# Fetching a norm weight's row on ScalarE's queue, with a buffer of ones for the first filling products

## The chip, the cores and the metric

The kernel runs on one core of a Trainium2 chip. The metric is the device time in microseconds of one execution, the median of several runs. A profile of one execution gives the times of single instructions, in microseconds from the start of its span.

## The reference

One step of a streaming encoder layer for 2048 new frames and 64 frames of a running stream, each of 1024 features. What matters here is its beginning, a norm and one wide projection:

```python
def rms_norm(x, g):
    xf = x.astype(jnp.float32)
    y = xf * lax.rsqrt(jnp.mean(xf * xf, axis=-1, keepdims=True) + EPS)
    return (y * g.astype(jnp.float32)).astype(x.dtype)
...
    aq, ak, av, ag, hq, hf, hi, hg = jnp.split(rms_norm(x, ln_g) @ w_in, SPLITS, axis=-1)
...
    o_a = attn_fn(heads(aq), k, v).reshape(B, T, W_A) * jax.nn.silu(ag)
    o_b, S = hgrn2_branch(hq, hf, hi, hg, lb, norm_g, s0)
    y = x + jnp.concatenate([o_a, o_b], axis=-1) @ w_out
```

Half of the projected features go through chunked attention, half through a gated linear recurrence. A second projection adds to the input, and a last norm follows. All data is 32 bits wide.

## The kernel before, in words

The frames are worked on in four blocks of 512 (the second carries the 64 frames of the running stream as well). For each block, the normed input is transposed into features by frames, split into a high part `xh` and a rest `xl`, and multiplied with 32 column groups of the input weights, each split likewise. The attention and the recurrence of a block run between its projections; the output projection follows at the end.

The order of every engine is written out by a planner in the kernel (`Plan`): a main program for TensorE yields after each product or two, and threads (loads, norms, splits, attention) go on when the planner's own clock `C.now` has reached the time that they wait for. The planner's clock only decides the order in which instructions are written; it isn't a time on the chip. Each engine executes its own list in order and waits on semaphores. Most instructions are recorded by one helper at line 266, so the profile is read by tiles.

The change lies in `program()`, in the first dozen microseconds:

- VectorE clears `g_in` (128 partitions by 1024), then SyncE fetches the input norm's weights, one row of 4 KB, into its first partition. The list of first loads stands in lines 2064 to 2074: two tiles of frames `xn` (128 by 1024, 512 KB each), the row, the first weights `wraw`, a third tile, the second weights, the fourth tile (in the room `kd`), the 4 KB of bounds `lbg`, and the third and fourth weights (in `kd` and `v`).
- Two products with a matrix of ones (lines 2112 to 2114) spread the row over all 128 partitions, one half into the bank `s` and one into the bank `pv`: the other partitions of `g_in` hold zeros, so the sum over partitions is the row.
- `x_tile` (line 542) takes the squares of a tile on ScalarE, makes the scale `rstd` of each frame there, scales the tile on VectorE by it and by the spread row (one half with `s`, one with `pv`), transposes its eight pieces on TensorE with the identity `ident`, four to a bank (`acc`, `tr`, `g`); `x_split` casts them into `xh` on ScalarE and puts the rest into `xl` on VectorE.
- GpSimd casts the first weights and takes their rests (`w<-wraw`), two column blocks at a time.
- `project` (line 732) multiplies: eight products of `xh` with the weights, eight of `xl` with them, eight of `xh` with the weights' rest.
- Until the row and the first tiles are there, TensorE is given filling products into the bank `g`, whose values are never read: `spinning()` (line 2101), seven ahead of the row and one wherever the planner finds nothing else (lines 2108 to 2118).

`C.breath` is a 128 by 128 buffer that GpSimd clears between long rows of its work, as a pause.

Of the kernel before, what the change touches and what calls it, by code (L numbers as in the profile page):

```python
# [8 lines left out]
F32 = mybir.dt.float32  # L9
# [8 lines left out]
P = 128  # L18
# [354 lines left out]
def hymba_step(  # L373
# [23 lines left out]
    nc = tc.nc  # L397
    C = Plan()
    act, dve, pool, pe, sp = (Queue(C, e, x) for e, x in (("A", nc.scalar), ("D", nc.vector), ("P", nc.gpsimd),
                                                          ("T", nc.tensor), ("S", nc.sync)))  # L400
# [4 lines left out]
    cst = ctx.enter_context(tc.tile_pool(name="cst", bufs=1))  # L405
# [7 lines left out]
    def T(pool_, shape, dt, tag, **kw):  # L413
        uid[0] += 1
        C.name(homes.get(id(pool_), ""), tag, kw.get("bufs") or 1, f"{tag}_{uid[0]}")
        return pool_.tile(list(shape), dt, tag=tag, name=f"{tag}_{uid[0]}", **kw)

    def psum(tag, shape=(P, 512), bufs=1):
        return T(ps, shape, F32, tag, bufs=bufs)
# [27 lines left out]
                                     ck=1, slot=4, x4=0, x5=0, rec=1).items()}  # L447


    ident = T(cst, [P, P], F32, "ident")  # L450
    make_identity(nc, ident)
    ones = T(cst, [P, P], F32R, "ones")
    mask = T(cst, [P, P], U32, "mask")
    eps_t = T(cst, [P, 1], F32, "eps")
    one_t = T(cst, [P, 1], F32, "one")
    C.breath = T(cst, [P, P], F32, "breath")
    reset = T(cst, [P, 512], F32, "reset")
    asb = [T(cst, [P, 4, P], F32, f"asb{i}") for i in range(2)]
    g_norm = T(cst, [P, NHB], F32, "gnorm")
# [54 lines left out]
    g_in = T(px, [P, D], F32, "gin")  # L514
# [16 lines left out]
    def x_rows(sb, c, rows):  # L531
        if c < WIN:
            tok = SUPER[sb][0] + c
            return x_prompt[tok : tok + rows, :]
        return x_sample[:rows, :]
# [1514 lines left out]
    def program():  # L2050
# [13 lines left out]
        for what, i in (("x", 0), ("x", 1), ("g", 0), ("w", 0), ("x", 2), ("w", 1), ("x", 3), ("b", 0), ("w", 2),  # L2064
                        ("w", 3)):
            if what == "g":
                sp.dma_start(g_in[0:1], ln_in_g.rearrange("(o d) -> o d", o=1))
            elif what == "b":
                sp.dma_start(lbg, lb_gamma)
            elif what == "x":  # L2070
                sp.dma_start(xr0[i], x_rows(0, i * P, P))
            else:
                sp.dma_start(wr0[i], w_in[order[i][1]].rearrange("p (k n) -> p k n", k=KT))
            landed[what, i] = C.dma()
        for i in range(4):
            raws[i] = (wr0[i], landed["w", i], "raw" if i < 2 else None)
        spin = psum("g")
# [1 line left out]
        tk["g"].take()  # L2079
        tk["s_ps"].take()  # L2080
        tk["pv"].take()
        C.now = 600.0
        C.free["P"] = 4000.0

        def first_x():
# [12 lines left out]
            yield lambda: 3 in w_at  # L2098
            tk["kv"].put()

        def spinning():
            pe.matmul(spin[:, :P], ident, ident, start=True, stop=True)
            C.now += 200.0

        C.spawn(first_x(), 0)
        C.spawn(forget_bounds(), 1)
        C.spawn(weights(), 2)
        for _ in range(7):
            spinning()
            yield None  # L2110

        for a in range(2):
# [1 line left out]
            yield None  # L2114
        have.add("gain")
        while "rows" not in have:
            spinning()
            yield None
        tk["g"].put()

# [1 line left out]
        for sb in range(nsb):  # L2122
# [6 lines left out]
            for u, (kind, g) in enumerate(JOBS[sb]):  # L2129
# [11 lines left out]
                if (kind[0], g) not in made:  # L2141
                    d, evs = made[kind[0], g] = (head_jobs if kind[0] == "h" else pair_jobs)(sb, g)
# [98 lines left out]
    def out_rows_a():  # L2241
# [12 lines left out]
        wo_load(6, halves_of(hi, lo))  # L2254

    C.main(program())
    C.drain()

# [57 lines left out]
```

## Time and profile before

| | |
|---|---|
| median of 3 runs | 1248.94 us (1248.63 to 1250.27) |
| the profiled execution | 1248.92 us |
| its span (first to last instruction) | 1247.2 us |
| TensorE busy | 1231.4 us, 99% of the span |
| VectorE, ScalarE, GpSimd busy | 887.9, 701.3, 371.6 us |
| first product of the projection | 12.39 us from the span's start |

In the profile PE is TensorE and PEld its weight loads, DVE is VectorE, ACT is ScalarE, POOL is GpSimd and SP is SyncE; SPq and ACTq are DMA issues of these two. A filling or a transposing product of 32-bit data is one `pe` call. In the profile a filling product and each half of the spreading show as two instructions (the seven calls are 14).

### The profile page before, as it was taken

Reading aid. Unit: us, or ns where it says so; the run is one execution under the profiler, and the core shown is the slowest. Engines: PE = TensorE matmul, PEld = TensorE weight load, DVE = VectorE, ACT = ScalarE, POOL = GpSimd, SP = SyncE. Lnnn points to the kernel's source line nnn. Section 1 sums busy time; section 2 is a strip of 40 time slices with the busy share of each in tenths; the row PEclk is TensorE's granted clock in tenths of the full one; section 3 lists DMA queues with packets and bytes.
Section 4 is the critical chain, followed back from the end, with each engine's and each line's share of the span. In section 5 each row is a group of like instructions: output and inputs, shape, how many; then the busy total and the mean of one; then the engine's idle time right before and its main releaser. Section 6 shows DMA issues by size and latency. Waiting matters only on the chain.

```text
span 1247.2 us, 22061 instructions
## 1 busy us (share of the span) xinstructions
PE 1231.4 (99%) x8060; PEld 1078.6 (86%) x8060; DVE 887.9 (71%) x1862; ACT 701.3 (56%) x1535; POOL 371.6 (30%) x698
## 2 busy tenths in 40 slices
PE   8999999999999999999999999999999999999997
PEld 7788887999999999998888888898888888888786
DVE  6678778776857678687584748683848574787886
ACT  6354546666656557575565657763636455643443
POOL 6757565111120210202533535100101204441110
PEclk9999999999999999999999999999999999999999
DMA  7788688635454554636859596846363656897331
GB/s 266 265 309 287 226 328 330 242 131 211 141 187 143 181 203 143 219 126 228 282 205 344 201 359 226 276 163 213 127 234 115 216 209 263 311 318 202 127 136 68
DMA packets 95406, 273.29 MB, mean 219 GB/s; under 512 B 10369, under 2 KB 43137, under 8 KB 77634
## 3 DMA queue, kind: packets, MB, share of 16 engines
q1 hardware_dynamic: 95154, 271.62, 61.9%
q8 instruction: 64, 1.05, 0.3%
q14 instruction: 44, 0.36, 0.1%
q10 hardware_dynamic: 144, 0.26, 0.1%
HBM read 188.23 MB, written 85.19 MB: 219 GB/s over the span
## 4 chain that ended last, share of the span: by engine, by line
PE 77%; DVE 5%; issue 2%; ACT 2%; DMA 1%; POOL 1%; SPq 0%; DVEq 0%; ACTq 0%; POOLq 0%
PE acc L266 55%; PE g L266 7%; PE tr L266 5%; PE pv L266 5%; PE s L266 5%; DVE xn L266 1%; DVE pr L266 1%; DMA xn<-in_x_prompt_dram 1%; DMA wraw<-in_w_in_dram 0%; POOL w L266 0%; ACT ck L266 0%; DVE q L266 0%; DVE mixa L266 0%; DVE k L266 0%; ACT sig L266 0%
## 5 line engine op out<-in xcount | busy, mean ns | idle before, releaser
L266 PE MATMUL acc<-xh,w 128*128 128x512 f32 (+2 forms) x2688 | 567.1, 349 | 1.7 <-ACT sig L266 0.8
L266 PEld LDWEIGHTS acc<-xh,w 128*128 128x128 f32 x2688 | 434.3, 189 | 52.7 <-DVE gq L266 1.1
L266 PE MATMUL acc<-xl,w 128*128 128x512 f32 (+2 forms) x1344 | 296.1, 350 | 0.0
L266 PEld LDWEIGHTS acc<-xl,w 128*128 128x128 f32 x1344 | 217.2, 189 | 24.7
L266 DVE CUSTOM_DVE_ANT_0 pr<-s,bias 128x640 f32<-128x640 f32 (+5 forms) x144 | 100.8, 704 | 34.2 <-PE s L266 33.7
L266 ACT ACTIVATE pr<-pr,nm 128x640 f32<-128x640 f32 (+4 forms) x132 | 100.7, 763 | 41.3 <-DVE nm L266 40.4
L266 ACT CAST ph<-tr 128x512 fp32r<-128x512 f32 (+3 forms) x176 | 88.3, 508 | 62.8 <-PE tr L266 33.7
L266 POOL TENSOR_TENSOR w<-wraw,w 128x256 fp32r<-128x256 f32 x120 | 105.2, 906 | 57.3 <-issue 22.4
L266 POOL TENSOR_TENSOR mixa<-mixa,sga 128x256 f32<-128x256 f32 (+1 forms) x36 | 28.2, 784 | 308.1 <-DVE mixa L266 266.9
L266 DVE TENSOR_TENSOR ph<-tr,ph 128x512 fp32r<-128x512 f32 (+3 forms) x176 | 100.6, 590 | 8.8 <-ACT ph L266 7.6
L266 PE MATMUL pv<-ph,v 128*128 128x256 f32 (+2 forms) x344 | 95.7, 370 | 0.5 <-DVE ph L266 0.5
L266 PE MATMUL tr<-ident,pr 128*128 128x128 f32 x580 | 90.6, 273 | 0.4 <-DVE sig L266 0.2
L266 PEld LDWEIGHTS tr<-ident,pr 128*128 128x128 f32 x580 | 71.0, 140 | 13.6 <-issue 2.2
L266 ACT ACTIVATE sig<-acc 128x256 f32<-128x256 f32 (+2 forms) x86 | 42.7, 497 | 61.8 <-PE acc L266 61.6
L266 DVE TENSOR_SCALAR pr<-pr,sm 128x640 f32<-128x640 f32 (+4 forms) x132 | 72.2, 547 | 4.7
L266 ACT COPY vT<-acc 128x512 f32<-128x512 f32 (+2 forms) x62 | 31.0, 500 | 75.6 <-PE acc L266 75.4
L266 DVE TENSOR_TENSOR mixa<-mixa,pv 64x256 f32<-64x256 f32 (+1 forms) x144 | 56.9, 395 | 21.0 <-ACT mixa L266 16.7
L266 PEld LDWEIGHTS pv<-ph,v 128*128 128x128 f32 x344 | 58.3, 189 | 7.2 <-DVE ph L266 0.9
L266 ACT ACTIVATE sig<-sig 128x512 f32<-128x512 f32 (+2 forms) x109 | 57.4, 528 | 9.9 <-DVE gk L266 7.2
L266 POOL TENSOR_TENSOR xn<-wraw,xn 128x256 fp32r<-128x256 f32 x48 | 36.6, 781 | 69.8 <-ACT xn L266 69.8
L266 PE MATMUL s<-kd,q 128*128 128x320 f32 (+3 forms) x232 | 56.8, 315 | 0.4
L266 PE MATMUL s<-kd,ql 128*128 128x320 f32 (+3 forms) x232 | 55.5, 309 | 0.0
(310 smaller groups left out, 2040.6 us busy)
## 6 DMA issues: line engine op xcount, KB each, us to landing
w<-wd SPq DMA_DIRECT2D x96, 1024.0 KB, 5.0
wd<-w SPq DMA_DIRECT2D x32, 1024.0 KB, 7.4
wraw<-in_w_in_dram SPq DMA_DIRECT2D x30, 512.0 KB, 5.5
wod<-xn SPq DMA_DIRECT2D x28, 512.0 KB, 5.8
xn<-in_x_prompt_dram SPq DMA_DIRECT2D x23, 512.0 KB, 6.1
bias<-biasd SPq DMA_DIRECT2D x12, 640.0 KB, 8.1
carry<-kd SPq DMA_DIRECT2D x12, 512.0 KB, 7.5
carry<-v SPq DMA_DIRECT2D x12, 512.0 KB, 5.3
```

The lines of the kernel that those rows point to most:

```text
L266: r = f(*args, **kw)
```

## The change

Three edits: the row's fetch goes to ScalarE's queue, without the planner's charge; the buffer `breath` is filled with ones as the first work of GpSimd and feeds the first seven filling products (the later ones still use the identity); the planner's clock starts the stage at 800 instead of 600.

```diff
+    C.breath = T(cst, [P, P], F32, "breath")
+    nc.gpsimd.memset(C.breath, 1.0)
     ident = T(cst, [P, P], F32, "ident")
     make_identity(nc, ident)
...
-    C.breath = T(cst, [P, P], F32, "breath")
...
             if what == "g":
-                sp.dma_start(g_in[0:1], ln_in_g.rearrange("(o d) -> o d", o=1))
+                nc.scalar.dma_start(g_in[0:1], ln_in_g.rearrange("(o d) -> o d", o=1))
...
-        C.now = 600.0
+        C.now = 800.0
...
-        def spinning():
-            pe.matmul(spin[:, :P], ident, ident, start=True, stop=True)
+        def spinning(a):
+            pe.matmul(spin[:, :P], a, a, start=True, stop=True)
             C.now += 200.0
...
         for _ in range(7):
-            spinning()
+            spinning(C.breath)
             yield None
...
         while "rows" not in have:
-            spinning()
+            spinning(ident)
             yield None
```

TensorE's list at its start, before. `g` is the bank of the filling products, `s` and `pv` take the spread row, `acc` and `tr` the transposed pieces of the first tile (`xn_170`) and the second (`xn_171`):

```order
L266 MATMUL g_185<-ident_69 128x128 x7
L266 MATMUL s_186<-gin_154,ones_74 128x512
L266 MATMUL pv_187<-gin_154,ones_74 128x512
L266 MATMUL g_185<-ident_69 128x128
L266 MATMUL acc_214<-ident_69,xn_170 128x128 x4
L266 MATMUL g_185<-ident_69 128x128
L266 MATMUL acc_223<-ident_69,xn_170 128x128 x4
L266 MATMUL g_185<-ident_69 128x128
L266 MATMUL tr_232<-ident_69,xn_171 128x128 x4
L266 MATMUL tr_237<-ident_69,xn_171 128x128 x4
L266 MATMUL acc_246<-xh_155,w_209 128x256 x8
```

The same place after the change, with the tiles numbered anew (the first tile is `xn_171`, the second `xn_172`):

```order
L266 MATMUL g_186<-breath_69 128x128 x7
L266 MATMUL s_187<-gin_155,ones_76 128x512
L266 MATMUL pv_188<-gin_155,ones_76 128x512
L266 MATMUL g_186<-ident_71 128x128 x3
L266 MATMUL acc_215<-ident_71,xn_171 128x128 x4
L266 MATMUL g_186<-ident_71 128x128
L266 MATMUL acc_224<-ident_71,xn_171 128x128 x4
L266 MATMUL g_186<-ident_71 128x128
L266 MATMUL tr_234<-ident_71,xn_172 128x128 x4
L266 MATMUL g_186<-ident_71 128x128
L266 MATMUL tr_243<-ident_71,xn_172 128x128 x4
L266 MATMUL acc_249<-xh_156,w_220 128x256 x8
```

The first seven fillers read the ones. Three fillers stand behind the spreading products where one stood, and one more stands between the second tile's two groups of transposes.

ScalarE's list at its start, after the change (the row's fetch is the third line; before it wasn't there):

```order
L2313 UNCONDITIONAL_BRANCH
L402 ACT_TABLE_LOAD
L2068 DMA gin_155<-in_ln_in_g_dram 1x1024
L266 ACTIVATE ck_199,ss_190<-xn_171 128x1024
L266 ACTIVATE rstd_201<-ss_190,eps_78 128x1
```

The fetch stands behind the table load and ahead of the first tile's squares, and it waits for VectorE's clearing of `g_in`, as SyncE's fetch did. On SyncE the row's fetch, third in the list before, is gone, and the first weights follow the two tiles at once. On GpSimd the memset of the ones is the first work. Behind these places, the lists of all engines hold the same instructions in the same order.

## The prediction

> **What bounds the kernel now.** I read the page first: busy shares, clock and the chain of work that ended last.
>
> ```profile
> span 1247.2 us, 22061 instructions
> PE 1231.4 (99%) x8060; PEld 1078.6 (86%) x8060; DVE 887.9 (71%) x1862; ACT 701.3 (56%) x1535; POOL 371.6 (30%) x698
> PE 77%; DVE 5%; issue 2%; ACT 2%; DMA 1%; POOL 1%; SPq 0%; DVEq 0%; ACTq 0%; POOLq 0%
> ```
>
> TensorE is busy 1231.4 of 1247.2 us, so whatever moves its first useful product moves the end. Only 15.8 us are idle, but busy is not useful: filling products (into `g`) count as busy. The order lists differ only in the first dozen microseconds, so the next view is the time line of that stretch (start, length, engine, instruction, idle before it and what ended that).
>
> ```profile
> 0.80 0.20 POOL masks.py:197 MEMSET ident<- 128x128 f32 x1 [0.29 <-POOLq L2303]
> 0.81 0.86 SPq L266 DMA_DIRECT2D xn<-in_x_prompt_dram  x2
> 0.81 1.28 ACT L402 ACT_TABLE_LOAD   x1 [0.81 <-PEq L2303]
> 1.08 0.29 POOL masks.py:199 TENSOR_SCALAR_AFFINE_SELECT ident<-ident 128x128 f32<-128x128 f32 x1
> 1.09 0.91 DVE L266 MEMSET gin<- 128x1024 f32 x1 [1.09 <-PEq L2303]
> 1.43 3.36 PE L266 MATMUL g<-ident 128*128 128x128 f32 x14 [1.43 <-POOL one L266]
> 2.03 0.31 SPq L266 DMA_DIRECT2D gin<-in_ln_in_g_dram  x1
> 2.38 0.36 SPq L266 DMA_DIRECT2D wraw<-in_w_in_dram  x1
> 5.55 2.05 PE L266 MATMUL s<-gin,ones 128*128 128x512 f32 x2 [0.76 <-DMA gin<-in_ln_in_g_dram]
> 5.61 0.20 ACT L266 ACTIVATE rstd<-rstd 128x1 f32<-128x1 f32 x1
> 6.17 1.06 ACT L266 ACTIVATE ck<-xn 128x1024 bf16<-128x1024 f32 x1 [0.36 <-DMA xn<-in_x_prompt_dram]
> 7.39 1.92 PE L266 MATMUL pv<-gin,ones 128*128 128x512 f32 x2
> 7.49 1.04 POOL L266 CAST w<-wraw 128x1024 fp32r<-128x1024 f32 x1 [3.92 <-DMA wraw<-in_w_in_dram]
> 7.68 0.20 ACT L266 ACTIVATE rstd<-rstd 128x1 f32<-128x1 f32 x1
> 7.71 0.75 DVE L266 SCALAR_TENSOR_TENSOR xn<-xn,rstd,s 128x512 f32<-128x512 f32 x1 [4.72 <-ACT rstd L266]
> 8.62 2.80 POOL L266 TENSOR_TENSOR w<-wraw,w 128x256 fp32r<-128x256 f32 x4
> 9.09 0.63 PE L266 MATMUL g<-ident 128*128 128x128 f32 x2
> 9.34 0.75 DVE L266 SCALAR_TENSOR_TENSOR xn<-xn,rstd,pv 128x512 f32<-128x512 f32 x1 [0.88 <-PE pv L266]
> 9.52 0.83 PE L266 MATMUL acc<-ident,xn 128*128 128x128 f32 x4
> 10.00 0.74 DVE L266 SCALAR_TENSOR_TENSOR xn<-xn,rstd,s 128x512 f32<-128x512 f32 x1
> 10.19 0.39 PE L266 MATMUL g<-ident 128*128 128x128 f32 x2
> 10.41 0.60 PE L266 MATMUL acc<-ident,xn 128*128 128x128 f32 x4
> 11.71 1.07 ACT L266 CAST xh<-tr 128x512 fp32r<-128x512 f32 x2
> 12.39 1.19 PE L266 MATMUL acc<-xh,w 128*128 128x256 f32 x8 [0.28 <-ACT xh L266]
> ```
>
> The first useful product starts at 12.39. Behind it stands this chain: the row lands (TensorE's wait for it ends at 5.55), two products spread it over all partitions into `s` and `pv`, VectorE scales the first tile's halves (7.71, 9.34) and the second tile's (10.00, 10.66), TensorE transposes, ScalarE casts, the projection begins. The row is what ends last: the first tile's scale was ready at 5.61 + 0.20 = 5.81, and its scaling began only at 7.71, when `s` was done.
>
> **TensorE's speed here.** The granted clock in the rows stands at 1.00 throughout, but the durations do not. Each spreading product is two instructions: 5.55 to 7.39 and 7.39 to 9.09, so about 0.85 us an instruction. A filling product took 0.48 us (14 instructions in 3.36) early and 0.22 late (10.19 to 10.41). So TensorE doubles its speed at about 9.5, after 3.9 us without a break since 5.55. The first stretch, 1.43 to 4.79, was 3.36 us long and did not do it. Unbroken work of more than 3.4 and at most 4.0 us is thus what these rows ask for.
>
> **The change, part by part.**
>
> *A buffer of ones for the first fillers.* TensorE started 0.06 after the identity was finished (1.08 + 0.29 = 1.37). Ones are a single memset, first on GpSimd: 0.80 + 0.20 = 1.00, so TensorE starts at 1.06, 0.37 earlier, and its seven fillers end at 1.06 + 3.36 = 4.42. The added 0.2 us moves all GpSimd work behind it, but the first thing that counts there waits for its weights until 7.49, so it is hidden. VectorE's cast of `ones` waits for its own memset to 2.00 and loses at most 0.1.
>
> *The row on ScalarE's queue.* It waits for the table load (0.81 + 1.28 = 2.09) and VectorE's memset (1.09 + 0.91 = 2.00), so it is issued at 2.1, no earlier than the 2.03 of now. What it leaves is SyncE's queue, where two tiles of 512 KB stand ahead of it; it took 3.5 us to land. How fast such a row lands on ScalarE's queue while the other is full is not in the trace. The nearest rows are these (KB each, us from issue to landing), from the last microseconds, and the packets of an early one:
>
> ```profile
> out_dram<-asb SPq DMA_DIRECT2D x1, 256.0 KB, 2.0
> out_dram<-pr ACTq DMA_DIRECT2D x1, 256.0 KB, 2.5
> DMA packets 101, 0.41 MB, mean 406 GB/s; under 512 B 2, under 2 KB 2, under 8 KB 101
> ```
>
> Packets are 4 KB (0.41 MB in 101), so the row is about one of them. Bounds: 2.0 us (lands at 4.1) and 3.5 as now (5.6). I take 2.2 to 2.5, near the ScalarE row: 4.3 to 4.6, as the fillers end. The spreading products then start at 4.4 to 4.5 instead of 5.55: **1.1 us gained**, and the 0.76 us hole between fillers and spreading is closed, or nearly. ScalarE's own issue (about 0.4 us) lies in its idle time before the first tile.
>
> *What the closed hole does.* TensorE works without a break from 1.06, so by the rule read above it speeds up 3.4 to 4.0 us later, at 4.5 to 5.1. The four spreading instructions then take between 4 x 0.43 and 0.7 slow plus 3.2 x 0.43, so they end near 6.3 to 6.5, not 9.09. From 9.09 to the first useful product TensorE, VectorE and ScalarE needed 3.3 us. The new order adds two fillers ahead of the transposes and one between the last two groups (3 x 0.22 = 0.66), while the one filler and the first group that were slow save 0.4. So 3.5 us, which would give 10.0.
>
> *What is late next.* The second tile's scale: it lands after 6 us and its factor is ready at 7.68 + 0.20 = 7.88, whatever the row does. Its scaling, now at 10.00, cannot begin before 7.9. That path gains 10.00 - 7.9 = **2.1 us**, and the first useful product stands at 12.39 - 2.1 = 10.3. The added fillers then lie in TensorE's waits for VectorE.
>
> *SyncE goes on.* The weights of the first projection are issued at 1.7, not 2.38. The queue carries some 400 GB/s without a pause, so they land when the two tiles ahead are through, about 7.4 as now: nothing gained, and nothing needed, since GpSimd's first weight parts end at 8.62 + 2.80 = 11.42 and TensorE loads its first columns that use the residues (the `x10` row below) from 14.32 on (12.2 then).
>
> Does the shift last? These are the early transfers that don't move with it:
>
> ```profile
> kd<-in_x_prompt_dram SPq DMA_DIRECT2D x1, 512.0 KB, 7.6
> lbg<-in_lb_gamma_dram SPq DMA_DIRECT2D x1, 4.0 KB, 7.2
> 3.72 0.45 SPq L266 DMA_DIRECT2D kd<-in_x_prompt_dram  x1
> 4.22 0.61 SPq L266 DMA_DIRECT2D lbg<-in_lb_gamma_dram  x1
> 13.71 0.15 DVE L266 TENSOR_TENSOR lmx<-lbg 128x4 f32<-128x4 f32 x1
> 14.30 1.04 ACT L266 ACTIVATE ck<-kd 128x1024 bf16<-128x1024 f32 x1
> 14.32 1.27 PEld L266 LDWEIGHTS acc<-xh,w 128*128 128x128 f32 x10
> ```
>
> The fourth tile lands at 3.72 + 7.6 = 11.3 and is used at 14.30 (12.2 then). The bounds land at 4.22 + 7.2 = 11.4 and are used at 13.71 (11.6 then): just free. A gain over 2.3 us would run into them. Later transfers are issued as buffers come free and move along, and behind 13 us both order lists are equal on every engine.
>
> **Sum.** The profiled execution took 1248.92 us, 1.72 outside its span, and the median of the runs shown is 1248.94, so they stand for each other. 1248.92 - 2.1 = **1246.8 us**. A measurement of this kernel tells about 0.2% from no change, 2.5 us, so the forecast itself is "within".
>
> **The rivals.**
>
> *The speed comes late (1.0 us gained, 1247.9).* One execution can't say whether 3.4 to 4.0 us is a fixed count. If TensorE speeds up only after the spreading products, they end at 4.5 + 0.1 + 4 x 0.85 = 8.0 and the product starts at 11.4 to 11.5. A small hole left at 4.4 to 4.8 would do the same. For it: a hole of 0.76 reset the count. Against: the speed would have to stay low through 6.9 us of unbroken work, 1.06 to 8.0, where 3.9 were enough before.
> The Trainium skill, "TensorE: Matmul & The Clock Gate", Part 1 (the HAM clock gate), says that the clock is raised after a busy window of about 3.4 us that runs free of the kernel's start; by it the rise falls anywhere from 4.5 to 7.9 here, an estimate, and the gain anywhere from 1.0 to the 2.1 of above. The trace agrees with a doubled rate after 3.4 to 4 us.
>
> *The row comes no earlier (0 gained, 1248.9).* All transfers run on the same 16 engines, and these are full (406 GB/s); if the row waits for the running tiles' share of an engine, it lands at 5.5 as now. TensorE then sits 1.1 us, its speed comes as now, and 0.4 saved on the slow parts does not arise, while the fillers add up to 0.6: 1248.9 to 1249.5. Against: packets of 4 KB leave an opening every 0.16 us on each engine (4 KB at 406/16 GB/s).
> The Trainium skill, "DMA: Bandwidth & Descriptors", section "Issuing engines are not separate DMA queues", speaks for this rival: transfers from several engines interleave on the same hardware and only the issuing time is saved. Its section "Queues, rings and completion order" lets each engine alternate between queues at packet bounds, which speaks for an early row; no row here shows a small transfer beside a full other queue.
>
> *Slower: SyncE's going on puts the weights ahead of the row.* If the row is served behind all that SyncE has issued by 2.1, the first weights too, it lands with them at 7.4. Decisive is a landing after about 5.8. The spreading then starts 1.9 later on a TensorE that has stood 3 us, and three slow fillers and slow transposes add some 1.1: +3.0, **1251.9**.
>
> *More than 2.5 us.* The second tile's path could run a little tighter than 2.1 (TensorE's own path allows 10.0, that is 2.4), and the wait of TensorE after the first projection's first weights could shrink too:
>
> ```profile
> 20.92 1.22 PE L266 MATMUL acc<-xh,w 128*128 128x256 f32 x8 [0.76 <-ACT sig L266]
> ```
>
> Half of this 0.76 and 2.3 at the start are 2.7: 1246.2.
>
> **How the numbers follow.** Forecast 0.48 (1246.3 to 1247.3, centre 1246.8, within 0.2%); late speed 0.14 (within); row no earlier 0.06 (within: 1248.9 to 1249.5); more than 2.5 us 0.26 (faster); slower 0.06. So faster 0.26, same 0.68, slower 0.06. The range 1246.0 to 1248.5 leaves out the two cases at 1248.9 and above, 0.12, and a little at the lower end.
>
> **What would show it.** In the profile after: fillers from about 1.06 on the ones buffer; the row's issue on ScalarE's queue at 2.1; the first spreading product at 4.4 to 4.6 with no wait, or almost none, ahead of it; the second pair of spreading instructions under 1 us; the second tile's scaling at 7.9, waiting for ScalarE's factor; the first projection product at 10.3; the wait on `sig` near 18.8; every later landmark about 2 us earlier. Wrong would be a wait for the row up to 5.5, slow spreading products to the end, VectorE waiting for the bounds at about 11.5, or a gain at 12 us that is gone by 40 us.

## The result and the profile after

| | before | after |
|---|---|---|
| median of all runs beside each other | 1247.47 us (1246.05 to 1250.27, 22 runs) | 1250.05 us (1247.64 to 1255.0, 22 runs) |
| ratio to before, 95% interval | | 1.0023 [1.0015, 1.0031] |
| the profiled execution, its span | 1248.92, 1247.2 us | 1249.68, 1247.7 us |
| first product of the projection | 12.39 us | 13.35 us |

The change makes the kernel slower, by 2.6 us where 2.1 us of gain were forecast. The page of the profile after, first its head and the engines' shares in the chain that ended last:

```profile
span 1247.7 us, 22074 instructions
PE 1231.4 (99%) x8066; PEld 1079.0 (86%) x8066; DVE 888.5 (71%) x1862; ACT 701.0 (56%) x1535; POOL 369.6 (30%) x699
PE 76%; DVE 5%; issue 2%; DMA 2%; ACT 1%; POOL 1%; SPq 0%; DVEq 0%; POOLq 0%; ACTq 0%
```

TensorE's busy time is that of before, and the DMA's share of the chain has grown from 1% to 2%. The time line of the start (start, length, engine, instruction, idle before it and what ended that):

```profile
0.80 0.20 POOL L451 MEMSET breath<- 128x128 f32 x1 [0.29 <-POOLq L2304]
1.06 3.35 PE L266 MATMUL g<-breath 128*128 128x128 f32 x14 [1.06 <-POOL breath L451]
1.71 0.43 SPq L266 DMA_DIRECT2D wraw<-in_w_in_dram  x1
2.03 0.52 ACTq L2068 DMA_DIRECT2D gin<-in_ln_in_g_dram  x1
5.71 0.20 ACT L266 ACTIVATE rstd<-rstd 128x1 f32<-128x1 f32 x1
6.32 2.04 PE L266 MATMUL s<-gin,ones 128*128 128x512 f32 x2 [1.91 <-DMA gin<-in_ln_in_g_dram]
7.31 0.20 ACT L266 ACTIVATE rstd<-rstd 128x1 f32<-128x1 f32 x1
7.82 1.04 POOL L266 CAST w<-wraw 128x1024 fp32r<-128x1024 f32 x1 [4.24 <-DMA wraw<-in_w_in_dram]
8.16 1.92 PE L266 MATMUL pv<-gin,ones 128*128 128x512 f32 x2
8.48 0.75 DVE L266 SCALAR_TENSOR_TENSOR xn<-xn,rstd,s 128x512 f32<-128x512 f32 x1 [5.50 <-PE s L266]
10.78 0.74 DVE L266 SCALAR_TENSOR_TENSOR xn<-xn,rstd,s 128x512 f32<-128x512 f32 x1
13.35 1.35 PE L266 MATMUL acc<-xh,w 128*128 128x256 f32 x8
```

The fillers start at 1.06 and the row is issued at 2.03, as forecast. But TensorE waits for the row until 6.32, not 4.4 to 4.6: 4.3 us after its issue, against 3.5 on SyncE's queue before. The DMA queues show the wait from the other side (`q1` is SyncE's queue, `q10` ScalarE's; packets, MB, share of the 16 engines): the first line is the stretch from 0 to 5 us, the other two that from 5 to 6.

```profile
q1 hardware_dynamic: 297, 1.09, 60.6%
q1 hardware_dynamic: 81, 0.33, 87.4%
q10 hardware_dynamic: 2, 0.00, 1.1%
```

The row's packet moved at 5.51, when SyncE's queue had moved 1.2 MB; the two tiles ahead of the row are 1.0 MB.

The hole in TensorE's work has grown from 0.76 to 1.91 us, and the spreading products run at the low speed (2.04 us a pair). The second tile's scale is ready at 7.31 + 0.20 = 7.51, but VectorE only gets to that tile at 10.78. So the first product is 0.96 us later than before (13.35 against 12.39): 0.77 by the row (6.32 against 5.55), and most of the rest behind the spreading, where TensorE works without a break and now has the added fillers in its list (9.87 to 13.35, which is 3.48 us, against 9.09 to 12.39, which is 3.30).

That explains 0.96 of 2.6 us. Behind the start this execution is about as long as that of before: span less first product is 1234.35 against 1234.81. The rest of the loss must lie in executions that went otherwise than these two; the profiled execution of before, 1248.92 us, is itself 1.45 us above the median of its 22 runs.

### The profile page after: what moved, and what is told of

It is laid out like the page before. It is cut to its first block, busy times and chain, and to the rows that moved or that the text cites. A ratio compares the mean times of both kernels' runs of the same rounds, so it can differ in the third digit from the quotient of the medians.

```text
span 1247.7 us, 22074 instructions
## 1 busy us (share of the span) xinstructions
PE 1231.4 (99%) x8066; PEld 1079.0 (86%) x8066; DVE 888.5 (71%) x1862; ACT 701.0 (56%) x1535; POOL 369.6 (30%) x699
## 4 chain that ended last, share of the span: by engine, by line
PE 76%; DVE 5%; issue 2%; DMA 2%; ACT 1%; POOL 1%; SPq 0%; DVEq 0%; POOLq 0%; ACTq 0%
PE acc L266 55%; PE g L266 6%; PE tr L266 5%; PE pv L266 5%; PE s L266 5%; DMA wraw<-in_w_in_dram 2%; DVE xn L266 1%; DVE pr L266 1%; POOL w L266 1%; DVE q L266 0%; DVE w L266 0%; DVE kd L266 0%; ACT ck L266 0%; DVE k L266 0%; DVE mixa L266 0%
```

## The experiments

Four things came with the change: the row's queue, SyncE going on without waiting, the buffer of ones, and more fillers behind the spreading products. The theory at first (A) was that the row lands later because of its queue; the rival (B) was that the ones or the added fillers cost. Each timed kernel was compared with runs of the kernel before beside it, 12 runs of its own and 23 or 35 of before. Medians are given, then the ratio with its 95% interval; 0.001 of it is 1.25 us.

### The queue alone

In the kernel before, the fetch moves to ScalarE's queue, with the planner's charge, so that every list keeps its order.

```diff
-                sp.dma_start(g_in[0:1], ln_in_g.rearrange("(o d) -> o d", o=1))
+                row = ln_in_g.rearrange("(o d) -> o d", o=1)
+                nc.scalar.dma_start(g_in[0:1], row)
+                C.charge("S", sp.cost("dma_start", [g_in[0:1], row], {}), [g_in[0:1]], [row])
```

> The kernel before with one edit: the row is fetched on ScalarE's queue (the planner is charged as before, so every list is otherwise the same). Theory Q (the row lands later on ScalarE's queue than behind the two tiles on SyncE's, because SyncE's next 512 KB transfers get ahead of it): the wait for the row ends at 6 to 7 us instead of 5.55, the time is 1 to 3 us longer than before and spreads more. Theory F (the queue is indifferent, the loss comes from the early start and the three added fillers): the wait ends at 5.5 or earlier and the time is within 0.5 us of before.

Measured: 1250.15 us (before beside it 1248.01), ratio 1.0017 [1.0007, 1.0027]. Its time line:

```profile
1.43 3.36 PE L266 MATMUL g<-ident 128*128 128x128 f32 x14 [1.43 <-POOL one L266]
6.38 1.10 PE L266 MATMUL s<-gin,ones 128*128 128x512 f32 x2 [1.59 <-DMA gin<-in_ln_in_g_dram]
11.22 1.35 PE L266 MATMUL acc<-xh,w 128*128 128x256 f32 x8
```

The row is used at 6.38 here too, and a loss of 2.1 us is here (0.9 to 3.4 by the interval): moving the fetch makes it, without the ones and the added fillers. Yet in this one profile the speed rose early (1.10 us a pair) and the first product came at 11.22, earlier than before. This execution took 1247.58 us, below the median of before: one profile is not the median.

### The ones alone

The changed kernel with the row back on SyncE's queue and the planner's clock at 600: before, but for the buffer in the first seven fillers.

```diff
-                nc.scalar.dma_start(g_in[0:1], ln_in_g.rearrange("(o d) -> o d", o=1))
+                sp.dma_start(g_in[0:1], ln_in_g.rearrange("(o d) -> o d", o=1))
...
-        C.now = 800.0
+        C.now = 600.0
```

> The kernel before with the buffer of ones for the first seven fillers, the row still on SyncE's queue, fillers in number and place as before. Theory Q: the row lands at 5.5 as before, only the hole ahead of the spreading grows from 0.76 to 1.1 us; time within 0.4 us of before. Theory F: the longer hole keeps TensorE slow for longer, 0.5 to 1.5 us slower.

Measured: 1248.12 us (before 1248.01), ratio 1.0 [0.999, 1.001]: no difference beyond 1.25 us.

```profile
5.42 2.05 PE L266 MATMUL s<-gin,ones 128*128 128x512 f32 x2 [1.00 <-DMA gin<-in_ln_in_g_dram]
12.33 1.19 PE L266 MATMUL acc<-xh,w 128*128 128x256 f32 x8 [0.28 <-ACT xh L266]
```

TensorE starts 0.37 earlier, waits 0.24 to 0.38 longer for the same row, and the product comes as before. So the part of rival B about the ones falls.

### The changed kernel without the added fillers

```diff
-                nc.scalar.dma_start(g_in[0:1], ln_in_g.rearrange("(o d) -> o d", o=1))
+                row = ln_in_g.rearrange("(o d) -> o d", o=1)
+                nc.scalar.dma_start(g_in[0:1], row)
+                C.charge("S", sp.cost("dma_start", [g_in[0:1], row], {}), [g_in[0:1]], [row])
...
-        C.now = 800.0
+        C.now = 600.0
```

> The changed kernel with the fillers behind the spreading as before (one, not three, and none between the last two groups of transposes). If the added fillers cost: 0.6 (fast) to 1.3 us (slow) less than the changed kernel. If they lie in waits: within 0.3 us of it.

Measured: 1249.61 us (before 1247.82), ratio 1.001 [0.9999, 1.002].

```profile
6.65 1.10 PE L266 MATMUL s<-gin,ones 128*128 128x512 f32 x2 [2.23 <-DMA gin<-in_ln_in_g_dram]
11.49 1.35 PE L266 MATMUL acc<-xh,w 128*128 128x256 f32 x8
1089.82 0.73 PE L266 MATMUL pv<-ph,v 128*128 128x512 f32 x2 [2.04 <-DVE ph L266]
```

By the median the loss is 1.8 us, about that of the changed kernel, though this interval takes in none. That the added fillers are not the main loss rests on the queue alone as well, which loses 2.1 us without them. They are not free: at the high speed, TensorE's stretch from the end of the spreading to the first product is 3.05 us here (8.44 to 11.49) and 3.31 with them (7.70 to 11.01 in the next kernel). (The third line is taken up at the end.)

### SyncE held, the row on ScalarE's queue

The changed kernel, in which SyncE also fetches the row, into a spare buffer that VectorE clears first: SyncE waits there as it did before. This kernel fetches the row twice.

```diff
+        spare = T(wk, [P, 2, 640], F32, "bias", bufs=1).rearrange("p a c -> p (a c)")
+        nc.vector.memset(spare[0:1, :8], 0.0)
...
                 nc.scalar.dma_start(g_in[0:1], ln_in_g.rearrange("(o d) -> o d", o=1))
+                sp.dma_start(spare[0:1, :D], ln_in_g.rearrange("(o d) -> o d", o=1))
```

> The changed kernel, and SyncE fetches the row as well, into a spare buffer, at the place and with the wait that it had before, so that the first weights are issued at 2.4 us again and not at 1.7. Theory W (the row on ScalarE's queue comes late because SyncE's going on puts the first weights, 512 KB, ahead of it): the wait for the row ends at 5.6 us or earlier, the first projection product near 12.4 or earlier, and the time comes within 1 us of before. Rival A (the row is late on ScalarE's queue whatever SyncE does): the wait ends at 6.2 to 6.4 us as in the changed kernel, and the time stays 1.5 to 3 us over before.

Measured: 1249.61 us (before 1247.82), ratio 1.0011 [0.9998, 1.0024].

```profile
2.03 0.52 ACTq L2070 DMA_DIRECT2D gin<-in_ln_in_g_dram  x1
2.40 0.36 SPq L266 DMA_DIRECT2D wraw<-in_w_in_dram  x1
5.91 1.10 PE L266 MATMUL s<-gin,ones 128*128 128x512 f32 x2 [1.50 <-DMA gin<-in_ln_in_g_dram]
1086.22 0.61 DVE L266 TENSOR_SCALAR pr<-pr,sm 128x640 f32<-128x640 f32 x1
```

With the weights issued at 2.40 again instead of 1.71, the row is used at 5.91: between the 5.41 to 5.55 of SyncE's queue and the 6.25 to 6.65 of ScalarE's with SyncE going on. Neither expectation has that. So roughly half of the delay comes with the weights that are issued ahead of the row, and half with ScalarE's queue itself. The row's own packet agrees: it moved at 4.99 here, when SyncE's queue had moved 1.1 MB, and at 5.39 to 5.82 in the six profiles with the row on ScalarE's queue and SyncE going on. The split rests on one profile, the second fetch of the row may have cost something, and the run times do not tell this kernel from the changed one.

### The row first

Two kernels fetch the row before all else on SyncE's queue. In the first no buffer is cleared, and the spreading products sum over one partition:

```diff
-        dve.memset(g_in, 0.0)
...
-            pe.matmul(gps[a], f32(ones), g_in[:, a * 512 : a * 512 + 512], start=True, stop=True)
+            pe.matmul(gps[a], f32(ones)[0:1], g_in[0:1, a * 512 : a * 512 + 512], start=True, stop=True)
```

> The kernel before with the row first in SyncE's list, ahead of the tiles, without VectorE's clearing; the spreading product takes only the first partition (one row of ones, same sums). Three more fillers stand behind it. If the landing of the row is what the start waits for: it lands at about 3 us, the spreading starts when the seven fillers end (4.5 to 4.8), the second tile's scale (7.9 plus about 0.3 for the later issue) is next: 0.7 to 2 us faster than before. If the row is not what counts: within 0.3 us, or slower by the 0.3 us of the tiles' later issue.

Measured: 1251.13 us (before 1248.01), ratio 1.002 [1.0007, 1.0032].

```profile
4.71 2.07 PE L266 MATMUL s<-gin,ones 1*128 1x512 f32 x2
14.63 1.60 PE L266 MATMUL acc<-xh,w 128*128 128x256 f32 x8
```

The row is there when the fillers end, there is no hole, and it is the slowest kernel of all: TensorE works without a break from 4.71 and stays at the low speed to about 14.3. In this profile, products over one partition did not raise the speed. In the second kernel the row lands in partition 96 and 97 partitions take part:

```diff
-        dve.memset(g_in, 0.0)
+        dve.memset(g_in[0:96], 0.0)
...
-            pe.matmul(gps[a], f32(ones), g_in[:, a * 512 : a * 512 + 512], start=True, stop=True)
+            pe.matmul(gps[a], f32(ones)[0:97], g_in[0:97, a * 512 : a * 512 + 512], start=True, stop=True)
```

> The kernel before with the row first in SyncE's list, into partition 96; VectorE clears only partitions 0 to 95, and the spreading product takes 97 partitions (same sums), so that the row waits for no clearing. Two more fillers stand behind the spreading. In row_first the one-partition products ran slowly to the end, and TensorE's speed rose only at 14 us. If products over one partition do not count as work for TensorE's speed: here the spreading starts at 4.6 to 4.8 without a hole, the speed rises between 4.7 and 8.3, the first projection product comes at 10.3 to 11.5, 0.8 to 2 us faster than before. If the late tiles were what cost row_first its time: slower than before by 1 us or more here too.

Measured: 1248.87 us (before 1247.82), ratio 1.0003 [0.9992, 1.0015].

```profile
4.57 1.23 PE L266 MATMUL s<-gin,ones 97*128 97x512 f32 x2
7.94 0.75 DVE L266 SCALAR_TENSOR_TENSOR xn<-xn,rstd,s 128x512 f32<-128x512 f32 x1 [0.20 <-ACT rstd L266]
10.13 1.36 PE L266 MATMUL acc<-xh,w 128*128 128x256 f32 x8
1086.76 2.17 DVE L266 TENSOR_SCALAR pr<-pr,sm 128x640 f32<-128x640 f32 x1
1087.70 0.74 POOL L266 TENSOR_TENSOR slot<-wraw,slot 128x256 fp32r<-128x256 f32 x1
1090.33 1.17 PE L266 MATMUL pv<-ph,v 128*128 128x512 f32 x2 [2.04 <-DVE ph L266]
```

This start is the one that the prediction described: row at 4.57, speed up, the second tile's scaling at 7.94 waiting for ScalarE's factor, first product at 10.13. But the speed rose at 4.97, at the end of a window (1.56 to 4.97) that was nearly all fillers over all partitions, so this profile does not show what products over 97 partitions do for it. Its 2.3 us, and the 0.8 to 2 us expected, were not seen in the median. This profiled execution took 1251.44 us; behind the first product it is 4.5 us longer than that of before, and its lower three lines show a part of that: VectorE's scaling of `pr` took 2.17 us instead of the 0.61 of the SyncE-held kernel, while GpSimd worked on, and TensorE then waited 2.04 us, against 0.50 in the kernel before:

```profile
1089.68 0.73 PE L266 MATMUL pv<-ph,v 128*128 128x512 f32 x2 [0.50 <-DVE ph L266]
```

### The hole, with the row where it was

Left open was where the part of the loss beyond the row's 0.85 us comes from. In the kernel with the ones alone, the number of first fillers sets how long the hole ahead of the spreading products is. Ten, then eleven, then five fillers instead of seven, the planner's clock set back or forward by as much, so that the rest of every list stays as before:

```diff
-        for _ in range(7):
+        for _ in range(10):
```

> As ones_only, with ten first fillers instead of seven, so that they last from 1.06 to about 5.5 and no hole is left ahead of the spreading. If unbroken work raises TensorE's speed (as the prediction read it), the spreading is fast in part or whole and the first projection product comes 0.5 to 2 us earlier: 0.5 to 2 us faster than before. If the speed does not depend on the hole: no change within 0.3 us.

> The same with eleven first fillers: they end at 5.3, the hole is 0.1 or less. Theory A: the speed rises early in nearly every execution, first product 10.2, median 1.5 below before (1246.5), ratio 0.999. Theory B: no gain over ten fillers (1247.3), ratio 1.0000 to 1.0002.

> The row on SyncE's queue as before, five first fillers on the buffer of ones instead of seven, all else in the order of before: the fillers end near 3.5, the row is used at 5.35 to 5.55 as before, and the hole ahead of the spreading products is 1.9 to 2.0 us long, as in the changed kernel, with no later row. Theory A (the changed kernel loses about 0.85 us by the later row, and the rest of its 2 us because the longer hole makes an early rise of TensorE's speed rarer or breaks it): about 1 us over before, ratio 1.0006 to 1.001, few runs below 1247. Theory B (the hole's length costs nothing, all of the loss comes with the queue): ratio 1.0000 to 1.0002, and as many runs below 1247 as before has (a third).

Ten fillers: 1247.3 us (before 1248.01), ratio 1.0002 [0.9991, 1.0012].

```profile
1.06 3.99 PE L266 MATMUL g<-breath 128*128 128x128 f32 x20 [1.06 <-POOL breath L451]
5.35 1.10 PE L266 MATMUL s<-gin,ones 128*128 128x512 f32 x2 [0.29 <-DMA gin<-in_ln_in_g_dram]
10.19 1.36 PE L266 MATMUL acc<-xh,w 128*128 128x256 f32 x8
```

Eleven: 1247.44 us (before 1248.35), ratio 0.9991 [0.9981, 1.0002]; no hole at all.

```profile
5.54 1.10 PE L266 MATMUL s<-gin,ones 128*128 128x512 f32 x2
10.38 1.36 PE L266 MATMUL acc<-xh,w 128*128 128x256 f32 x8
```

Five: 1249.71 us (before 1248.35), ratio 1.0009 [1.0001, 1.0018].

```profile
5.45 2.04 PE L266 MATMUL s<-gin,ones 128*128 128x512 f32 x2 [1.89 <-DMA gin<-in_ln_in_g_dram]
11.86 1.35 PE L266 MATMUL acc<-xh,w 128*128 128x256 f32 x8
```

With the row at the same 5.35 to 5.55, a hole of 1.89 us instead of 0.62 to 0.76 costs 1.4 us by the medians (0.1 to 2.2 by the interval). So the longer hole itself costs, though TensorE has nothing useful to do in it. That its absence brings something is not shown: the medians are 0.7 and 0.9 lower, both intervals take in no gain, and the ratio of the ten is above 1. Nor is the cost to be seen in the one profile with five fillers, whose first product came at 11.86, ahead of the 12.25 to 12.81 of the three profiles of before; it stands in the run times. The other way round, the changed kernel with twelve first fillers (the row late, the hole small); the three added fillers are gone from it:

```diff
-        C.now = 800.0
+        C.now = -200.0
...
-        for _ in range(7):
+        for _ in range(12):
```

> The changed kernel with twelve first fillers on the ones instead of seven, so that they last from 1.06 to about 6.3, when the row is there; the later fillers are as in the kernel before. Theory C (a late row costs its 0.8 us once, and the rest of the loss is TensorE's slow speed after the hole): the spreading is fast in most executions, first product near 11.2, time 1 to 2.5 us shorter than the changed kernel, near before. If the hole does not matter: within 0.5 us of the changed kernel.

Measured: 1248.57 us (before 1247.82), ratio 1.0003 [0.9991, 1.0014].

```profile
6.43 1.10 PE L266 MATMUL s<-gin,ones 128*128 128x512 f32 x2 [0.66 <-DMA gin<-in_ln_in_g_dram]
11.27 1.34 PE L266 MATMUL acc<-xh,w 128*128 128x256 f32 x8
```

This kernel and the changed one without the added fillers differ in the five first fillers alone, and were timed beside the same runs of before: the five take the loss from 1.8 to 0.75 us. Those 0.75 fit the row's 0.9 us, but their interval (-1.1 to 1.75 us) takes in none as well.

### Both kernels again

> The kernel before, unchanged, timed against itself. Theory A (each execution's start is a draw: TensorE's speed rises at boundaries 3.41 us apart whose phase is free): the ratio's interval takes in 1; the profile's spreading products take either 2.05 us (late rise, first product near 12.4) or 1.10 us (early rise, first product near 10.5 to 11.3); the row is used at 5.3 to 5.6 whichever it is. Rival B (the speed's rise is fixed by the program): 2.05 us again, first product within 0.2 of 12.39. The 2.0 us wait of TensorE near 1088 us is seen in about 2 of 10 profiles so far; by A it may come here too, with the span less the first product near 1238 instead of 1234 to 1235.5.

> The kernel before, unchanged, one further profile. Theory A: early or late rise of TensorE's speed, with the row used at 5.3 to 5.6 either way. Rival B: spreading products of 2.05 us and the first product within 0.2 of 12.39 again.

> The changed kernel, unchanged, timed again. If its loss is the later row alone (0.9 to 1.0 us later use): ratio near 1.0008 to 1.001. If late rises of TensorE's speed are more frequent because the hole before the spreading products is 1.9 instead of 1.0 us: ratio near 1.002 as before, and the row used at 6.3 to 6.7 with spreading products of 2.05 us in most profiles.

> The changed kernel, unchanged, one further profile. Theory A: the row used at 6.3 to 6.7; the first product near 11.3 with an early rise of TensorE's speed, near 13.4 with a late one. Rival B (fixed by the program): first product within 0.2 of 13.35 again.

Before against itself: 1248.24 and 1247.99 us, ratio 1.0003 [0.9993, 1.0013]. The changed kernel: 1249.83 us, ratio 1.0015 [1.0005, 1.0025]. One further profiled execution of each took 1248.92 us (before) and 1249.67 us (changed). First the second profile of before, then the second profile of the changed kernel:

```profile
5.41 2.04 PE L266 MATMUL s<-gin,ones 128*128 128x512 f32 x2 [0.62 <-DMA gin<-in_ln_in_g_dram]
12.25 1.19 PE L266 MATMUL acc<-xh,w 128*128 128x256 f32 x8 [0.27 <-POOL w L266]
```

```profile
6.25 1.10 PE L266 MATMUL s<-gin,ones 128*128 128x512 f32 x2 [1.97 <-DMA gin<-in_ln_in_g_dram]
7.18 1.66 PE L266 MATMUL pv<-gin,ones 128*128 128x512 f32 x2
9.91 1.06 PE L266 MATMUL acc<-ident,xn 128*128 128x128 f32 x4
11.03 0.60 PE L266 MATMUL acc<-ident,xn 128*128 128x128 f32 x4
13.01 1.36 PE L266 MATMUL acc<-xh,w 128*128 128x256 f32 x8
```

The row's place repeats: 5.55, 5.41 and 5.41 in the three profiles of before, 6.32, 6.25 and 6.31 in those of the changed kernel. The speed doesn't. In the last fence it is high at 6.25 (1.10 us for the first two instructions of the spreading), falls within the next two (1.66), is low at 9.91 (1.06 us for four transposes) and high again at 11.03 (0.60 for four). It had risen early and was lost again.

### When the speed rises

The traces record the moments at which TensorE's clock changes, and nothing ahead of the first one (so the 1.00 that a profile's rows give before it is no measurement). They lie whole multiples of 3.413 us apart within an execution, at a phase that differs from execution to execution. Cutting the start of each of the sixteen profiles into windows of 3.413 us that end at such a moment, and adding up TensorE's idle time in each, gives this (us; a change happens at a window's end):

| kernel | window | idle in it | speed behind it |
|---|---|---|---|
| before | 3.16 to 6.57, then 6.57 to 9.98 | 0.76, then 0 | low, then high |
| before, second | 3.01 to 6.42, then 6.42 to 9.83 | 0.62, then 0 | low, then high |
| before, third | 0.76 to 4.17, then 4.17 to 7.59 | 0.67, then 0.63 | low, low (high at 11.0) |
| the ones alone | 3.16 to 6.58 | 1.00 | low (high at 9.99) |
| ten fillers | 0.82 to 4.23, then 4.23 to 7.64 | 0.24, then 0.29 | high, stays high |
| changed | 3.38 to 6.79, then 6.79 to 10.20 | 1.91, then 0 | low, then high |
| changed, second | 0.61 to 4.02, then 4.02 to 7.43 | 0.46, then 1.96 | high, then low (high at 10.85) |
| changed, third | 0.78 to 4.19, then 4.19 to 7.61 | 0.29, then 1.94 | high, then low (high at 11.02) |
| queue alone | 1.29 to 4.70, then 4.70 to 8.11 | 0.14, then 1.59 | high, stays high |
| without added fillers | 1.71 to 5.12, then 5.12 to 8.53 | 0.71, then 1.53 | high, stays high |
| SyncE held | 0.89 to 4.30, then 4.30 to 7.72 | 0.17, then 1.50 | high, stays high |
| eleven fillers | 1.61 to 5.02 | 0 | high, stays high |
| five fillers | 1.81 to 5.22, then 5.22 to 8.63 | 1.65, then 0.23 | low, then high |
| changed, twelve fillers | 1.39 to 4.80, then 4.80 to 8.21 | 0, then 0.66 | high, stays high |
| row in partition 96 | 1.56 to 4.97 | 0 | high, stays high |
| row first (one partition) | 4.05 to 7.47, then 7.47 to 10.88 | 0, then 0 | low, low (high at 14.29) |

A window with up to 0.46 us of idle time raised the speed each time, one with 1.0 us or more never did, and between 0.62 and 0.76 it went both ways, four times low and once (0.71) high; the row-first kernel, with products over one partition from 4.71 to 8.42, is apart. A window with 1.94 or 1.96 took the raised speed away, one with 1.59 or less did not. The same count over the whole length of the sixteen traces, which the table does not show, draws this line closely: no window with up to 1.91 us of idle time took the raised speed away, and every one with 1.94 or more did, the two behind the waits near 1090 (2.04) among them. The Trainium skill, "TensorE: Matmul & The Clock Gate", Part 1 (the HAM clock gate), states such a free-running window of 3413 ns; these profiles agree with it, and they add how much idle time a window bears.

So an execution of before is a draw. An estimate from the table: a window raises the speed early if it has at most 0.5 us of idle time, and with fillers from 1.43 to 4.79 its end must fall between 4.3 and 5.3, which is 1.0 of 3.41, or 28%. Of the 138 runs of before that stood beside the others, 37 (27%) lie below 1247.0 us, unevenly (3 of 23 in one comparison, 10 of 22 in another; of the 12 further ones that were timed against it, one); none of the 35 of the changed kernel do. There the fillers end at 4.42, ends between 4.0 and 4.9 raise the speed, but those before 4.4 are followed by a window that holds the whole hole and loses it again: 0.5 of 3.41, or 15%, remain. Six of its 35 runs (17%) lie at 1248.40 us or below, and the next at 1249.11. That the run times fall into these groups for this reason is argued from the shares: no profile of before shows an early rise. The windows and the row's places are shown, and the price of the longer hole within 1.1 us to either side.

## Why the prediction was wrong

- **Fillers on the ones at 1.06, row issued at 2.1:** right (1.06 and 2.03). The earlier start was harmless.
- **"I take 2.2 to 2.5, near the ScalarE row":** this is the step that failed. The row took 4.2 to 4.6 us from its issue to its use (6.25 to 6.65 in all six profiles on that queue with SyncE going on), outside the bounds of 2.0 to 3.5. The row of the last microseconds, 2.5 us, was issued at 1243.74, beside a single transfer of 256 KB on SyncE's queue (issued at 1243.53); at 2.03 three transfers of 512 KB, the two tiles and the first weights, stood there. In the trace of the changed kernel that queue's packets of the first 14 us are two, both between 5 and 6 (the row's 4 KB at 5.5): for 3.5 us after its issue nothing of the row moved, while SyncE's queue was being served. The term was taken from a row at the wrong end of the kernel, and its upper bound was the fetch as it was, as if another queue could not make it later.
- **"SyncE goes on ... nothing gained, and nothing needed":** its cost was missed. With SyncE held the row was used at 5.91 instead of 6.25 to 6.65. The rival "SyncE's going on puts the weights ahead of the row" had this mechanism, its point (a landing after 5.8) and the sign; it had a chance of 0.06 and a price of 3.0 us, of which the row and the hole made about 2. By the SyncE-held profile only about half of the delay comes this way.
- **"What the closed hole does":** the sign of the hole was right, but the change did not close it, it made it 1.9 us. What was read as "more than 3.4 and at most 4.0 us" of unbroken work is a window with a phase of its own, as the rival "the speed comes late" had it from the Trainium skill. The reading itself was off, too: by the clock's record the speed rose at 9.98, not at 9.5, 4.4 us behind the start at 5.55.
- **"What is late next", second tile's scale, first product at 10.3:** right where the row did come early and the speed rose early (7.94 and 10.13 in the kernel with the row in partition 96). The chain behind the row was sound, and so were the 3.5 us from the spreading to the first product (3.48 measured).
- **The base:** the profiled execution of before, 1248.92 us, was one of the late-speed draws, as were its two repeats; the median of 3 runs that the sum starts from, 1248.94, became 1247.47 over 22 runs. If the lower quarter of its runs are early rises, as argued above, these already had most of the gain that closing the hole was to bring.

The account of the loss, by medians: 1.4 us by the longer hole (the kernel with five fillers), 0.75 by the later row (the changed kernel with twelve), together 2.1, against 2.6 in the first comparison and 1.84 in the second (1249.83 less 1247.99). The intervals of the two are 1.1 and 1.4 us to either side, so the split is rough, and what is left is less than these runs can resolve. No kernel here beats before beyond its interval; eleven fillers on the ones, with the row on SyncE's queue, comes nearest (0.9991 [0.9981, 1.0002]).

**What stays open.** In two profiles of sixteen (row in partition 96, and changed without added fillers) TensorE waits 2.04 us for `ph` near 1090, where it waits 0.5 otherwise, and the clock's record shows the low speed for one window of 3.41 us behind it. Span less first product is then 1237.5 to 1239.3 instead of 1233.9 to 1235.5. In run times above 1250 this may be a good part. Whether an earlier start makes it more frequent, which would explain why the 2.3 us of the kernel with the row in partition 96 did not reach its median, was not settled.

## What to carry to other kernels

A small fetch on another engine's queue was not ahead of a full queue here: ask what is issued before it on every queue, and take its landing time from a row in which the other queue is as full as in the place that it goes to. A hole in TensorE's early work can cost more than the work it lacks, because a window with a hole keeps the low speed; fill it up to the moment at which the data is there, with products over all partitions. Where the start is a draw, read several profiles before a microsecond of one of them is priced.

## What the runs showed of the hardware

- The raised speed fell behind a window of 3.41 us with 1.94 us or more of idle time and held with up to 1.91, in all sixteen traces.
- A 4 KB fetch on ScalarE's queue beside a full SyncE queue took 4.2 to 4.6 us from issue to use, on SyncE's own queue behind two 512 KB tiles 3.3 to 3.5. The Trainium skill, "DMA: Bandwidth & Descriptors", section "Issuing engines are not separate DMA queues", says that transfers of all engines interleave on the same 16 DMA engines and that only issuing time is saved; the trace agrees in that the second queue brought no earlier use (6.25 to 6.65 against 5.41 to 5.55 us). Its section "Queues, rings and completion order", by which each DMA engine takes turns between the queues, would have let the row through early; this row's packet moved 3.5 us after its issue (5.5 less 2.03), and the measurement decides. What held it in those 3.5 us is not in the trace.
- Products over one partition left TensorE at the low speed through windows without any idle time (4.05 to 10.88 in the one profile of the row-first kernel, such products from 4.71 to 8.42). Whether 97 partitions raise it is not shown: the speed rose at 4.97, behind fillers over all partitions.
- VectorE's 0.61 us scaling of `pr` took 2.17 us beside GpSimd's back-to-back work, and TensorE's wait grew by 1.5 us behind it, in two of the sixteen profiles; in the others it took 0.61 to 0.66 with the same list on GpSimd. That VectorE waited for GpSimd there is argued from the two rows; no run took GpSimd's work away.
